# A hybrid encoder in fp32 on one core: the first output product in another PSUM bank, and loads, strips and stores put in another order

## The chip, the cores and the metric

One core of one Trainium2 chip. The metric is the device time of one execution in microseconds, the median of several runs. TensorE (PE, with its weight loads PEld) multiplies, VectorE (DVE) and ScalarE (ACT) work element by element, GpSimd (POOL) reduces over partitions, and SyncE (SP) issues the DMAs, in order, from one queue.

## The reference, cut to what matters

```python
def encoder_layer(h, norm_w, w_in, q_norm_a, k_norm_a, q_norm_b, k_norm_b, rpb, w_out, rope_tabs):
    B, N, _ = h.shape
    u = rms_norm(h, norm_w) @ w_in.astype(h.dtype)
    qa, ka, va, za, qb, kb, vb, zb = jnp.split(u, split_points(), axis=-1)
    qa = apply_axial_rope(rms_norm(qa.reshape(B, N, N_HEADS_A, HEAD_DIM), q_norm_a), rope_tabs)
    ka = apply_axial_rope(rms_norm(ka.reshape(B, N, N_KV_A, HEAD_DIM), k_norm_a), rope_tabs)
    va = va.reshape(B, N, N_KV_A, HEAD_DIM)
    ya = global_gqa(qa, ka, va) * jax.nn.silu(za)
    ...
    yb = neighbourhood_attention(qb, kb, vb, rpb) * jax.nn.silu(zb)
    y = jnp.concatenate([ya, yb], axis=-1) @ w_out.astype(h.dtype)
    return h + y
```

It is applied to a prompt of 1024 tokens and a sample of 256, each behind 16 meta tokens; the model has 2048 columns, 8 global heads (2 for K and V) and 8 local ones of 128 columns, all fp32. Global attention is softmax over all tokens, local attention over a window of 8 rows by 16 columns of a 64-wide grid, with a bias and the meta tokens.

## The kernel before, in words

Each fp32 operand is split into a high and a low fp32r half (`split`: ScalarE casts, L62; VectorE subtracts, L63), and a product is three matmuls (high by high, high by low, low by high).

*Projections.* A strip is one head's 128 columns of `w_in`. `strips` runs over 4 groups c of 4 row tiles kt; for each it loads the weights (tile wr, L190), splits them and multiplies (L211 to L213), for each block b of columns. Chunk 1 is 512 tokens: the sample, the meta tokens and the first 240 of the prompt. Chunk 2 is the other 784, in blocks of 512 (tiles x) and 272 (tiles xb), for which `load_all_x` (L145) loads all of x and keeps it split. A strip's sums lie in pool pp, four PSUM banks. They are read out by `qk_evac`, `v_rows`, with transposes on TensorE into pool tp, one bank (`v_turn` L261 and `rows_out` L502, copied out in L504 and L509), or `z_evac` (its first read is L267).

*Chunk 1* (L576) ends with the joint V and z strip of the last local head, whose rows are transposed in three turns through tp: the meta rows, split into vm (L63) and stored to vmd, the sample's rows, and the prompt's rows. vm is loaded again by `load_vm` for the values of that head. *Chunk 2* (L698) issues the loads of x, the rope tables (`consts`, L163) and the first k (`k_first`, L709), and begins with the joint strip of global K and V. In its global part two strips and the four query blocks of a head follow each other, and one strip of a local head fills in. Then `fill(len(late))` runs the other 24 late strips, in the order V, K, Q, z of each head; `run_due` is called at every second c, 48 times, and issues what `local_heads` has put at that place: loads of a head, the scores of a block, its values. `put_y` stores a block of y in L328. The last head's loads of k and q come due at place 46 of 48, its v and z follow the last strip, and its scores and values run between the first products.

*Output.* `outproj` (L1008) works through seven products of half-size matrices, 5 token tiles by 2 column blocks each: step n is 24 matmuls (`products`, L963) into pool pq, four banks that take over those of pp. w_out's operands take over the buffers of x (`w_load` L938: ww in xb; `w_operand` L949: wm in xa), and y's those of the strips' weights. From the second product on, `in_order` fixes the instructions of each engine in the order of the program. `load_y` and `make_y` get the y of tile m; from m = 10 on it is a sum of two loads (yr L904, ysum L930).

Apart from that, a planner orders instructions by the order of the program, by what is ready in its own model of time, and by the places where `issue_after`, `high_priority` or a dependency written by hand says otherwise. A pool with n buffers makes a tile wait for the release of the one n before.

## Time and profile before

| | us |
|---|---|
| median of 3 runs | 2173.62 (2173.07 to 2177.45) |
| profiled execution | 2173.82 |
| its span, first to last instruction | 2172.0 |
| first matmul; last strip matmul of chunk 1 starts | 5.35; 606.28 |
| last matmul of the strips starts | 1770.03 |
| first product starts | 1773.37 |

The mean granted TensorE clock is 0.999. A row of the timeline gives start, length, engine, line, operation, output<-inputs, sizes and count; a bracket gives the idle time of the engine before it and what ended it. A row of the waits gives who waited for whom, the total, the number and the longest. The time of a matmul in a row overlaps the next one's, so intervals are counted from start to start.

### The profile page before, as it was taken

To read this page: it belongs to the slowest core of one execution; us is meant where nothing else is said; L and a number is where in the kernel's file an instruction comes from. 1 tells how busy PE (TensorE), PEld (TensorE's weight loads), DVE (VectorE), ACT (ScalarE), POOL (GpSimd) and SP (SyncE) were. 2 spreads that over 40 slices of the span, in tenths; PEclk is the share of its full clock that TensorE was granted. 3 is DMA by queue.
4 is the path that set the end of the run, shared out by engine and by line. 5 is a ranking of instruction groups with operands and counts; after the bars stand their busy time and mean duration, and the time that the engine had idled before them with its cause. 6 is when DMAs were issued, how large, how long until landed. Compare 5 with 4: busy or idle time off the path is not lost.

```text
span 2172.0 us, 34106 instructions
## 1 busy us (share of the span) xinstructions
PE 2154.0 (99%) x11736; PEld 1879.0 (87%) x11736; DVE 1648.2 (76%) x2991; ACT 1113.5 (51%) x2294; POOL 523.4 (24%) x249
## 2 busy tenths in 40 slices
PE   9999999999999999999999999999999999999999
PEld 7888888888888999999999999989898988888887
DVE  8687976787864899997789988688777777455763
ACT  7556544555554666665666666444443464232230
POOL 1232422222311233231143224333333222000000
PEclk9999999999999999999999999999999999999999
DMA  8767889988554333334233344654433364663663
GB/s 301 222 198 230 281 285 322 348 276 264 176 187 145 103 110 106 116 115 139 98 115 98 109 131 143 188 160 139 135 124 121 125 202 133 219 241 102 232 224 107
DMA packets 263614, 383.83 MB, mean 177 GB/s; under 512 B 45040, under 2 KB 113296, under 8 KB 263440
## 3 DMA queue, kind: packets, MB, share of 16 engines
q1 hardware_dynamic: 263440, 381.65, 53.6%
q8 instruction: 92, 1.51, 0.3%
q14 instruction: 82, 0.67, 0.1%
HBM read 281.01 MB, written 100.38 MB: 176 GB/s over the span
## 4 chain that ended last, share of the span: by engine, by line
PE 90%; DVE 3%; DMA 3%; ACT 1%; issue 1%; SPq 1%; POOL 1%; DVEq 0%; ACTq 0%; POOLq 0%
PE pp L211 20%; PE pp L212 20%; PE pp L213 20%; PE pq L971 5%; PE pq L969 5%; PE pq L970 5%; PE sp L447 2%; PE po L481 1%; PE sp L343 1%; PE sp L342 1%; PE sp L341 1%; PE po L381 1%; PE po L382 1%; PE po L383 1%; PE tp L502 0%
## 5 line engine op out<-in xcount | busy, mean ns | idle before, releaser
L211 PE MATMUL pp<-x,wh 128*128 128x512 f32 (+1 forms) x1664 | 656.7, 396 | 5.4 <-ACT wh L62 5.3
L213 PE MATMUL pp<-x,wl 128*128 128x512 f32 (+1 forms) x1664 | 649.1, 390 | 0.0
L212 PE MATMUL pp<-x,wh 128*128 128x512 f32 (+1 forms) x1664 | 648.4, 390 | 0.0
L213 PEld LDWEIGHTS pp<-x,wl 128*128 128x128 f32 x1664 | 313.1, 188 | 62.3 <-DVE wl L63 0.9
L211 PEld LDWEIGHTS pp<-x,wh 128*128 128x128 f32 x1664 | 313.3, 188 | 61.8 <-ACT wh L62 6.3
L212 PEld LDWEIGHTS pp<-x,wh 128*128 128x128 f32 x1664 | 313.5, 188 | 52.6
L228 POOL PARTITION_ALL_REDUCE m<-ms x78 | 232.5, 2981 | 365.1 <-ACT ms L226 303.4
L63 DVE TENSOR_TENSOR wl<-wr,wh 128x512 fp32r<-128x512 f32 (+1 forms) x290 | 213.8, 740 | 126.0 <-ACT wh L62 103.2
L62 ACT CAST wh<-wr 128x512 fp32r<-128x512 f32 (+1 forms) x290 | 174.3, 606 | 216.8 <-PE pp L212 196.4
L310 POOL PARTITION_ALL_REDUCE tot<-a x80 | 177.1, 2214 | 445.2 <-DVE a L307 430.2
L212 PE MATMUL pp<-xb,wh 128*128 128x272 f32 x832 | 240.1, 289 | 0.0
L211 PE MATMUL pp<-xb,wh 128*128 128x272 f32 x832 | 239.6, 288 | 0.0
L213 PE MATMUL pp<-xb,wl 128*128 128x272 f32 x832 | 239.1, 287 | 0.0
L969 PE MATMUL pq<-wm,yh 128*128 128x512 f32 x560 | 219.2, 391 | 4.1 <-DVE z L267 3.1
L971 PE MATMUL pq<-wm,yl 128*128 128x512 f32 x560 | 218.9, 391 | 0.0
L970 PE MATMUL pq<-wm,yh 128*128 128x512 f32 x560 | 218.4, 390 | 0.0
L292 POOL PARTITION_ALL_REDUCE ma<-m x80 | 106.8, 1335 | 446.3 <-DVE m L290 441.7
L211 PEld LDWEIGHTS pp<-xb,wh 128*128 128x128 f32 x832 | 156.5, 188 | 7.3
L212 PEld LDWEIGHTS pp<-xb,wh 128*128 128x128 f32 x832 | 156.4, 188 | 7.1
L213 PEld LDWEIGHTS pp<-xb,wl 128*128 128x128 f32 x832 | 157.4, 189 | 0.1
L969 PEld LDWEIGHTS pq<-wm,yh 128*128 128x128 f32 x560 | 105.5, 188 | 26.4 <-ACT wm L62 3.2
L971 PEld LDWEIGHTS pq<-wm,yl 128*128 128x128 f32 x560 | 105.4, 188 | 22.3 <-DVE yl L63 0.4
(207 smaller groups left out, 3844.2 us busy)
## 6 DMA issues: line engine op xcount, KB each, us to landing
wr<-in_w_in SPq DMA_DIRECT2D x414, 256.0 KB, 3.4
wld<-wl SPq DMA_DIRECT2D x132, 256.0 KB, 4.3
wl<-wld SPq DMA_DIRECT2D x132, 256.0 KB, 3.1
yr<-yd SPq DMA_DIRECT2D x35, 512.0 KB, 5.2
wq<-in_w_out SPq DMA_DIRECT2D x64, 256.0 KB, 5.3
td<-wq SPq DMA_DIRECT2D x64, 256.0 KB, 4.3
ww<-td SPq DMA_DIRECT2D x64, 256.0 KB, 5.5
ww<-in_w_out SPq DMA_DIRECT2D x48, 256.0 KB, 5.1
```

Source lines behind the costliest of these rows:

```text
L62: self.hi = nc.scalar.copy(hi, full).ins
L63: return nc.vector.tensor_tensor(out=lo, in0=full, in1=hi.bitcast(F32), op=ALU.subtract).ins
L211: nc.tensor.matmul(p[:, :n], wh[:, k, :], xh[:, :n], start=first, stop=False)
L212: nc.tensor.matmul(p[:, :n], wh[:, k, :], xl[:, :n], start=False, stop=False)
L213: self.lastmm = nc.tensor.matmul(p[:, :n], wl[:, k, :], xh[:, :n], start=False, stop=last).ins
L228: nc.gpsimd.partition_all_reduce(m2[:], ms[:], P, RED.add)
L292: nc.gpsimd.partition_all_reduce(ma[:], m1[:], P, RED.max)
L310: nc.gpsimd.partition_all_reduce(tot[:], a1[:], P, RED.add)
L447: nc.tensor.matmul(dst, k[:, o:o + P], qfv[:, a:e, :], start=True, stop=True)
L969: nc.tensor.matmul(ps[:], yh, wh, start=k == 0, stop=False)
L970: nc.tensor.matmul(ps[:], yh, wl, start=False, stop=False)
L971: self.lastmm = nc.tensor.matmul(ps[:], yl, wh, start=False, stop=k == 7).ins
```

## The change

- Step 0 of the output product takes its PSUM tile from tp in place of pq.
- The last head's late strips run in the order K, Q, V, z; its k and q come due at place 44, its v at 46, its z after the strips. The loads of v and z are two functions now.
- The last strip, z, runs its two column blocks in turned order in every group c, and evacuates them so.
- Each local head's store of y gets a dependency on the last matmul before the next `run_due`; pool y has two buffers in chunk 2. Sl moves from pool sm (two buffers) into pool t, which gets a seventh.
- In chunk 2 the rope tables and the first k are issued on SP behind the first load of the last x; the weights of the first strip's groups 1, 2 and 3 and of the next strip's group 0 behind the loads of x of kt 3, 7, 11 and 15.
- The transposes of chunk 1's last strip are ordered behind the first block of 24 matmuls of chunk 2.
- y of tile 10 is loaded from step 16 on (before: step 18).

```diff
@@ load_all_x
                 with self.tc.issue_after(self.early):
-                    nc.sync.dma_start(r, self.x2d[kt][:, o:o + n])
+                    self.xload.setdefault(kt, nc.sync.dma_start(r, self.x2d[kt][:, o:o + n]).ins)
...
+        self.behind = [None] + [self.xload[c] for c in range(WCH - 1, KT, WCH)]
         for d, c in self.consts:
-            nc.sync.dma_start(d, c)
+            with self.tc.issue_after(self.xload[KT - 1]):
+                nc.sync.dma_start(d, c)
@@ strips
+            behind = self.behind.pop(0) if self.behind else None
             for s, _, _ in jobs:
-                with tc.high_priority(offset=self.woff):
+                with tc.high_priority(offset=self.woff), tc.issue_after(behind) if behind else nullcontext():
...
-            for b in range(len(jobs[0][1])):
+            nb = len(jobs[0][1])
+            for b in range(nb)[::-1] if self.turn else range(nb):
...
+                if self.second and self.turned:
+                    for i in self.turned:
+                        tc.add_manual_dep(i, self.lastmm.name, mybir.DependencyInfo(
+                            mybir.DependencyClass.NoSync, mybir.DependencyReason.DATA), reason="turned")
+                    self.turned = None
...
+    def turn_ins(self, i):
+        if not self.second:
+            self.turned.append(i)
...
     def run_due(self):
+        if self.late:
+            self.tc.add_manual_dep(self.late.pop(0), self.lastmm.name, mybir.DependencyInfo(
+                mybir.DependencyClass.Sync, mybir.DependencyReason.DATA), reason="late store")
@@ v_turn (rows_out in the same way)
-            self.nc.tensor.transpose(tp[:m, i, :], vt[:, o:o + m], self.ident[:])
+            self.turn_ins(self.nc.tensor.transpose(tp[:m, i, :], vt[:, o:o + m], self.ident[:]).ins)
@@ meta_scores
-        sm, sl = (self.sm.tile([M3, QB], F32, tag=n, name=n) for n in ("Sm", "Sl"))
+        sm = self.sm.tile([M3, QB], F32, tag="Sm", name="Sm")
+        sl = self.t.tile([P, QB], F32, tag="t", name="Sl")[:M3]
@@ put_y
-        nc.sync.dma_start(ydst, y[:].rearrange("p (g r) -> p g r", g=ydst.shape[1]))
+        self.ystore = nc.sync.dma_start(ydst, y[:].rearrange("p (g r) -> p g r", g=ydst.shape[1])).ins
@@ chunk1, before its last joint strip
+                self.turned = []
                 (v, vm), z = pr(vj, zj)
@@ chunk2
-            nc.sync.dma_start(k[:, :, :C1P].bitcast(F32), self.kd[g][:, :, :C1P])
-            nc.sync.dma_start(m.bitcast(F32), self.kd[g][:, :, C1P:])
+            with self.tc.issue_after(self.xload[KT - 1]):
+                nc.sync.dma_start(k[:, :, :C1P].bitcast(F32), self.kd[g][:, :, :C1P])
+                nc.sync.dma_start(m.bitcast(F32), self.kd[g][:, :, C1P:])
...
-                for p, (o, n) in zip(ps, BL):
+                for p, (o, n) in list(zip(ps, BL))[::-1 if self.turn else 1]:
...
         def values(h, b):
             next(blocks.pop((h, b)), None)
+            self.late.append(self.ystore)
...
-                    put(max(o + 5, 8 * h), load_vz, h + 1)
-            put(LATE - 2, load_kq, NH - 1)
+                    put(max(o + 5, 8 * h), load_v, h + 1)
+                    put(max(o + 5, 8 * h), load_z, h + 1)
+            put(LATE - 4, load_kq, NH - 1)
+            put(LATE - 2, load_v, NH - 1)
...
-            late += [v_rows_of(VB + h, 2 + h), qk_late(KB + h, kwb, self.k2d[2 + h]), qk_late(QB_ + h, qwb, self.q2d[8 + h]),
-                     z_late(ZB + h, self.zd[8 + h])]
+            v = [v_rows_of(VB + h, 2 + h)]
+            kq = [qk_late(KB + h, kwb, self.k2d[2 + h]), qk_late(QB_ + h, qwb, self.q2d[8 + h])]
+            late += (kq + v if h == NH - 1 else v + kq) + [z_late(ZB + h, self.zd[8 + h])]
...
-        fill(len(late))
-        load_vz(NH - 1)
+        fill(len(late) - 1)
+        self.turn = True
+        fill(1)
+        load_z(NH - 1)
@@ products
+        if first:
+            ps = self.tp.tile([P, 4, P], F32, tag="tp", name="pq")[:].rearrange("p a b -> p (a b)")
+        else:
+            ps = self.pq.tile([P, FB], F32, tag="pq", name="pq")[:]
@@ outproj
                 (load_y, make_y)[b](m + 1)
+                if m + 2 == 2 * NT:
+                    load_y(m + 2)
...
-            ps = self.products([ws[q, 8 * b + k] for k in range(8)], ys[m])
+            ps = self.products([ws[q, 8 * b + k] for k in range(8)], ys[m], n == 0)
@@ build
-                work = (("s", 5), ("ph", 2), ("sm", 2), ("mx", 2), ("t", 6))
+                work = (("s", 5), ("ph", 2), ("sm", 2), ("mx", 2), ("t", 7))
...
-                for name, bufs in (("k", 1), ("v", 1), ("tab", 1), ("q", 1), ("z", 1), *work, ("y", 1), ("qf", 1)):
+                for name, bufs in (("k", 1), ("v", 1), ("tab", 1), ("q", 1), ("z", 1), *work, ("y", 2), ("qf", 1)):
```

More of the change, by code (lines that the diff above doesn't have):

```diff
@@ L1 @@
-from contextlib import ExitStack
+from contextlib import ExitStack, nullcontext
 import numpy as np
@@ L145, in load_all_x @@
     def load_all_x(self):
-        nc = self.nc
+        nc, self.xload = self.nc, {}
         for kt in range(KT):
@@ L501, in rows_out @@
                 m = min(P, n - x)
-                nc.tensor.transpose(tp[:m, i, :], vt[:, x:x + m], self.ident[:])
+                self.turn_ins(nc.tensor.transpose(tp[:m, i, :], vt[:, x:x + m], self.ident[:]).ins)
             f = len(full)
@@ L577, in chunk1 @@
         nc, io = self.nc, self.io
-        self.due = iter(())
+        self.due, self.late, self.turn, self.behind, self.turned = iter(()), [], False, [], []
         self.woff, self.second, self.projected, self.sums = 0, False, 0, self.w_sums()
@@ L820, in run, with load_v, load_z @@
                 self.attend(q[:, :, c], z[:, c], keys, km, v, vm[:], self.yd[0][:, 2 * b:2 * b + 2, h, :])
-        kq, vz, blocks = {}, {}, {}
+        kqs, vs, zs, blocks = {}, {}, {}, {}
         def load_kq(h):
-            kq[h] = k_load(2 + h), self.bias_table(h, "bt", (3, 384)), q_load(8 + h)
-        def load_vz(h):
-            vz[h] = v_windows(h), z_load(8 + h)
+            kqs[h] = k_load(2 + h), self.bias_table(h, "bt", (3, 384)), q_load(8 + h)
+        def load_v(h):
+            vs[h] = v_windows(h)
+        def load_z(h):
+            zs[h] = z_load(8 + h)
         def scores(h, b):
-            (k, km), tab, (q, qf) = kq[h]
-            (v, vm), z = vz[h]
+            (k, km), tab, (q, qf) = kqs[h]
+            (v, vm), z = vs[h], zs[h]
             blocks[h, b] = self.attend_strip(q, qf, strips_of(z[:])[:, :, 64 * b:64 * b + 64], k, km, v[b], vm[:], tab, b,
@@ L838, in values @@
             next(blocks.pop((h, b)), None)
+            self.late.append(self.ystore)
         def local_heads():
             places = [[] for _ in range(LATE)]
-            seq = (values, load_vz, scores, load_kq)
+            seq = (values, load_v, load_z, scores, load_kq)
             def put(n, f, *a):
@@ L880, in chunk2 @@
                 fill(FILL)
-        load_kq(0)
-        load_vz(0)
+        for f in (load_kq, load_v, load_z):
+            f(0)
         self.due = iter(local_heads())
-        fill(len(late))
-        load_vz(NH - 1)
+        fill(len(late) - 1)
+        self.turn = True
+        fill(1)
+        load_z(NH - 1)
         self.due = iter([[(0, f, (NH - 1, b)) for f, b in ((values, n - 2), (scores, n)) if 0 <= b < 4] for n in range(6)])
@@ L961, in x_load, with products @@
         return o
-    def products(self, ws, y):
+    def products(self, ws, y, first):
         nc = self.nc
-        ps = self.pq.tile([P, FB], F32, tag="pq", name="pq")
+        if first:
+            ps = self.tp.tile([P, 4, P], F32, tag="tp", name="pq")[:].rearrange("p a b -> p (a b)")
+        else:
+            ps = self.pq.tile([P, FB], F32, tag="pq", name="pq")[:]
         for k in range(8):
@@ L968, in products @@
             yh, yl = (a[k // WCH][:, k % WCH, :] for a in y)
-            nc.tensor.matmul(ps[:], yh, wh, start=k == 0, stop=False)
-            nc.tensor.matmul(ps[:], yh, wl, start=False, stop=False)
-            self.lastmm = nc.tensor.matmul(ps[:], yl, wh, start=False, stop=k == 7).ins
-        return ps[:]
+            nc.tensor.matmul(ps, yh, wh, start=k == 0, stop=False)
+            nc.tensor.matmul(ps, yh, wl, start=False, stop=False)
+            self.lastmm = nc.tensor.matmul(ps, yl, wh, start=False, stop=k == 7).ins
+        return ps
     def out_sums(self, p, i, ps, o):
```

## The prediction

> **What bounds the kernel now.** I read the page first, then who TensorE waited for, then the stretches around each wait.

> ```profile
> span 2172.0 us, 34106 instructions
> ...
> PE 2154.0 (99%) x11736; PEld 1879.0 (87%) x11736; DVE 1648.2 (76%) x2991; ACT 1113.5 (51%) x2294; POOL 523.4 (24%) x249
> ```

> TensorE is busy for 2154.0 of 2172.0 us, so anything that is not a TensorE wait or a slowed matmul is worth nothing. The view of waits, TensorE alone (waiting engine and line, what ended the wait, total us, times, longest):

> ```profile
> PE pp L211 <- ACT wh L62: 5.3, 1, 5.3
> PE pq L969 <- DVE z L267: 3.1, 1, 3.1
> PE po L381 <- ACT ph L62: 1.6, 1, 1.6
> PE tp L261 <- DVE vm L63: 1.5, 1, 1.5
> PE sm_ps L280 <- DVE mx L351: 1.1, 2, 0.5
> PE pq L969 <- ACT yh L62: 1.0, 1, 1.0
> ```

> The first is the start of the program; the third and fifth belong to attention of chunk 1 and of the global heads, of which the diff moves one small tile (Sl) and nothing that is waited for. Three remain: L969 behind the last z evacuation, L261 behind the split of vm, L969 behind yh. What can be won is at these three places.

> **Place 1, the first product step** (the timeline of TensorE; start, length, what, and in brackets the idle time before it).

> ```profile
> 1769.90 0.29 PE L212 MATMUL pp<-xb,wh 128*128 128x272 f32 x1
> 1770.03 0.28 PE L213 MATMUL pp<-xb,wl 128*128 128x272 f32 x1
> 1773.37 0.77 PE L969 MATMUL pq<-wm,yh 128*128 128x512 f32 x1 [3.06 <-DVE z L267]
> ...
> 1776.90 0.40 PE L969 MATMUL pq<-wm,yh 128*128 128x512 f32 x1
> 1777.13 0.40 PE L970 MATMUL pq<-wm,yh 128*128 128x512 f32 x1
> ...
> 1780.34 0.60 PE L447 MATMUL sp<-qfull,kfull 128*128 128x128 f32 x4
> ...
> 1781.37 0.37 PE L281 MATMUL sp<-q,km 128*112 128x256 f32 x1 [0.31 <-DVE q L63]
> ```

> Matmuls overlap, so I count from start to start: 0.13 us for 272 columns (1769.90 to 1770.03), 0.23 us for 512 (1776.90 to 1777.13). The last projection matmul starts at 1770.03, the first product at 1773.37: 3.34 - 0.13 = 3.2 us lost. The step's 24 matmuls then take 1780.34 - 1773.37 = 6.97 us instead of 24 x 0.23 = 5.5, another 1.5. The stretches of time say why (length, each engine's busy time and instructions, then granted clock, DMA share and GB/s):

> ```profile
> 1770.00:1773.30 3.30, 0.31 (x3) 0.10 (x1) 3.30 (x7) 2.96 (x6) 0.00 (x0) 0.94 1.03 383
> 1773.30:1776.30 3.00, 2.93 (x7) 2.41 (x8) 2.85 (x5) 3.00 (x7) 0.00 (x0) 0.50 0.81 308
> ```

> After the idle 3 us the granted clock is 0.50 for the whole of the next 3. The 1.5 us hang on the wait and go with it. Last come 0.3 us in which the scores of the last head wait for q.

> What the change does here: step 0 (n == 0) writes the bank of the transposes instead of the first of the four banks that the projections give back, so it no longer waits for z to be read out of that bank. It needs that bank free, its operands, and then bank pq for step 1.

> The bank: the last V strip now ends one strip before the end, so its transposes stand in the z strip. How long they take is shown by the same head's V strip where it stands now (VectorE, then ScalarE):

> ```profile
> 1708.15 0.69 DVE L254 TENSOR_TENSOR vt<-pp,rb 128x512 f32<-128x512 f32 x1
> ```

> ```profile
> 1717.03 0.25 ACT L509 COPY vl<-tp 16x128 f32<-16x128 f32 x1
> ```

> From the first vt to the last copy out of the bank: 9.1 us. A strip is 48 x (0.23 + 0.13) = 17.3 us by the intervals above, so the bank is free some 8 us before step 0. If that cover were gone, step 0 would wait as now (a rival).

> The operands: VectorE has the low halves of w_out and y to make.

> ```profile
> 1772.54 0.69 DVE L267 TENSOR_TENSOR z<-pp,rb 128x512 f32<-128x512 f32 x1
> ...
> 1777.60 0.68 DVE L63 TENSOR_TENSOR wm<-ww,wm 128x512 fp32r<-128x512 f32 x1
> ...
> 1779.40 0.43 DVE L267 TENSOR_TENSOR z<-pp,rb 128x272 f32<-128x272 f32 x1
> ```

> The last of 16 wm is done at 1778.28. Unstalled, step 0 runs from 1770.2 to 1775.7, the scores of the last head to about 1777.0, and step 1 takes its last weight 21 x 0.23 = 4.8 us later, at 1781.8: 3.5 us to spare even at today's times. They will be earlier: Q's evacuation and the split of q leave this stretch for the strip before, V puts less work on VectorE, and with the blocks turned round the 272-column blocks of x, whose buffers the w_out loads take over, come free 12 x 0.23 = 2.8 us sooner per group of four; the 512-column ones come free 12 x 0.13 = 1.6 us later, but only the casts behind the loads need them. Turning costs no matmul. With Q a strip (17 us) earlier, the 0.3 us wait for q goes too.

> Step 1 now takes the first of pq's four banks, the one that step 0 waits for today, so z's 512-column block must be read by 1777.0. Today that block comes first, is complete at about 1770.0 - 12 x 0.13 = 1768.5, and is read from 1772.54, 4.0 us later. Turned, it is complete at 1770.3 and by the same delay read out by 1775.0, 2 us in time. I take no wait; the far bound is the place of today's second z block, done at 1779.83, a wait of 2.8.

> Sum of place 1: 3.2 + 1.5 + 0.3 = **5.0 us**, at least 2.2.

> [...]

> **Place 2, where chunk 2 starts.**

> ```profile
> 607.80 0.28 PE L261 MATMUL tp<-ident,vt 128*16 128x128 f32 x1
> 609.59 0.44 PE L261 MATMUL tp<-ident,vt 128*128 128x128 f32 x2 [1.51 <-DVE vm L63]
> ```

> The two transposes share one bank; the second waits until VectorE has split vm. The change orders all transposes of this strip behind the first 24 matmuls of chunk 2 (K and V, four kt, 512 columns: 5.5 us), and puts the loads of x ahead of k, of the rope tables and of later weights on SP. What TensorE has at 607.8 instead: 24 matmuls of 272 columns, whose x landed earlier, 3.1 us; then the 512-column ones as x arrives. ScalarE's rows for the casts of x:

> ```profile
> 609.18 0.72 ACT L159 ACTIVATE x<-x,nw 128x512 fp32r<-128x512 f32 x1 [0.61 <-DMA x<-x2d]
> ...
> 613.88 0.72 ACT L159 ACTIVATE x<-x,nw 128x512 fp32r<-128x512 f32 x1 [2.83 <-DMA x<-x2d]
> ```

> The first x is cast at 609.90 and TensorE would reach it at 610.9: covered. The third is late now because stores of vm and two weight loads stand ahead of it on SP; the stores move behind the transposes and the loads behind x. I take the full **1.5 us**. If the third x stays where it is, TensorE runs out at 610.9 + 12 x 0.23 = 613.7, and idles until 614.6, and as long again if the fourth follows as late, 1.8 us in place of 1.5: bounds -0.3 and +1.5. What moves back on SP: k and rope, first used in evacuations some 35 us later (two strips), which hides them; two weight loads by two issues, with 5.5 + 3.1 us of matmuls ahead of their use. The store of vm and its reload move some 5.5 us later, ahead of the last sample head's values; these are placed later by as much, and nothing of chunk 2 needs them soon.

> **Place 3, the third pass of products.**

> ```profile
> 1905.26 0.39 PE L971 MATMUL pq<-wm,yl 128*128 128x512 f32 x1
> 1906.67 0.50 PE L969 MATMUL pq<-wm,yh 128*128 128x512 f32 x1 [1.02 <-ACT yh L62]
> 1907.00 0.40 PE L970 MATMUL pq<-wm,yh 128*128 128x512 f32 x1
> 1907.39 0.50 PE L971 MATMUL pq<-wm,yl 128*128 128x512 f32 x1
> ```

> Three intervals take 2.13 us instead of 0.69: 1.4 lost. The cause is upstream on VectorE:

> ```profile
> 1889.20 1.23 DVE L930 TENSOR_TENSOR ysum<-yr 128x1024 f32<-128x1024 f32 x1 [4.58 <-DMA yr<-yd]
> ```

> VectorE stands 4.58 us for y of tile 10, with 16 wm and the next ysum queued behind it. The change issues this load at step 16 instead of 18, two steps or 11 us earlier. The queue moves up by up to 4.58 us, over three times what TensorE lost: **1.4 us**. Below, 0: it would take a load that, issued 11 us earlier, still kept VectorE waiting all 4.58 us. The order of instructions is fixed here by hand, so nothing else moves.

> **What costs nothing.** Late y stores: a store on SP waits for a later matmul; behind it stand weight loads. Between 1326 and 1733 TensorE is busy all the time,

> ```profile
> 1326.00:1733.00 407.00, 407.00 (x2445) 367.11 (x2444) 312.70 (x664) 187.01 (x421) 138.69 (x74) 1.00 0.45 144
> ```

> although SP already waits 84.4 us in all with these stores at its head:

> ```profile
> SPq L328 <- DVE y L327: 84.4, 42, 5.2
> ```

> The second y buffer and the seventh t are paid for with the two buffers of Sl; off TensorE's path either way: 0, bounds -1.1 (a pair of 0.5 waits for mx more) and +1.1 (both gone).

> **Sum.** 5.0 + 1.5 + 1.4 = 7.9 us off the profiled execution's 2173.8 (its span of 2172.0 and 1.8 around it) gives 2165.9; that execution stands 0.2 above the median of the runs, so as a median **2165.7 us**.

> **Rivals.** (a) *The wait moves to step 1*: VectorE comes to z's 512-column block as late as to today's second block. For it: VectorE is busy for 3.30 of 3.30 us there. Against: Q's work is gone from the stretch. 2.8 back: 2168.5, with half clock again, 1.5 more, 2170.0. (b) *x is the wait at chunk 2's start*: place 2 gives nothing or loses 0.3: 2167.2 to 2167.5. For it: the casts waited 2.83 us for x. Against: what stood ahead of it moves. (c) *The bank of the transposes isn't free*, so step 0 starts as late as today: 5.0 back, 2170.7. For it: V's evacuation now competes with the w_out splits. Against: 8 us of slack. (d) *Slower*: from 1326 on, 28 late stores hold SP until the matmul they are tied to, weights behind them come late, and TensorE waits once per store. It decides from 7.9 / 28 = 0.28 us per store; at 0.5, the longest wait for mx, it costs 14: 2179.7. For it: SP is in order. Against: the row of full TensorE under 84.4 us of held SP.

> **How the numbers follow.** Forecast 0.54, (b) 0.15, (a) 0.13, (d) 0.10, (c) 0.08. A measurement of this kernel can tell about 0.2%, 4.3 us, from no change: faster means below 2169.3. The forecast and (b) lie there nearly whole (0.67), (a) by half (0.07): 0.74. Slower is (d): 0.10; the rest, 0.16, within. The range begins at 2163.5 (the forecast less 1.1 for mx and 1.2 for other small waits) and ends at 2171.5, above (a) and (c); (d) is left out, and a tenth for what I haven't thought of.

> **What would show it.** Step 0 starting at about 1768.7 right behind the last z matmul, granted clock 1.00 through the stretch, no L447 or L281 wait; no wait at L261 and none for x around 608; no wait for yh in the third pass and none of VectorE for yr. A wait for z at step 1, one for x at L211, or any TensorE wait between 1326 and 1733 would make it wrong.

## The result

| | median, us (range) | runs |
|---|---|---|
| before, same chip | 2175.48 (2172.71 to 2178.41) | 20 |
| changed | 2172.49 (2170.73 to 2176.40) | 20 |
| predicted | 2165.7 (2163.5 to 2171.5) | |

The ratio is 0.9986, 95% interval 0.998 to 0.9992: 3.0 us faster, or 0.14%, where 7.9 us were forecast. The direction was right, the size was not. The profiled execution of the changed kernel took 2173.16 us, 0.7 more than its median; the one of before lies at the low end of its runs. So the traces differ by less than the medians, and are read for places, not for their total.

The page, and TensorE's waits (waiting engine and line, what ended the wait, total us, times, longest):

```profile
span 2171.4 us, 34104 instructions
...
PE 2154.0 (99%) x11736; PEld 1879.1 (87%) x11736; DVE 1647.0 (76%) x2991; ACT 1117.0 (51%) x2294; POOL 526.5 (24%) x249
```

```profile
...
PE tp L519 <- ACT wm L62: 3.9, 1, 3.9
...
PE pp L215 <- ACT x L159: 1.1, 1, 1.1
PE tp L519 <- DVE vt L270: 0.5, 1, 0.5
```

The waits that the prediction set out to remove are gone: the products' for z and for yh (L969), chunk 2's for vm (L261) and the scores' for q; with them went the scores' for mx (L280). In their place stand one for x and one, longer than any of them, at the transposes of the last V strip. The changed kernel's lines lie 4 to 31 further down: 211 to 213 are 215 to 217, 254 is 270, 261 is 277, 502 is 519, 504 is 521, 969 to 971 are 1000 to 1002.

**The new stand.** The timeline around it, all engines (start, length, engine, line, what; idle time before in brackets):

```profile
1752.38 0.32 SPq L821 DMA_DIRECT2D qfull<-q2d  x1
...
1757.41 0.28 PE L215 MATMUL pp<-xb,wh 128*128 128x272 f32 x1
1757.89 1.04 ACT L62 CAST q<-qfull 128x1024 fp32r<-128x1024 f32 x1 [3.47 <-DMA qfull<-q2d]
1758.84 0.61 ACT L62 CAST wh<-wr 128x512 fp32r<-128x512 f32 x1
1758.97 1.23 DVE L63 TENSOR_TENSOR q<-qfull,q 128x1024 fp32r<-128x1024 f32 x1 [3.56 <-ACT q L62]
1759.36 0.58 ACT L521 COPY vl<-tp 128x512 f32<-128x512 f32 x1
...
1760.11 0.69 DVE L63 TENSOR_TENSOR wl<-wr,wh 128x512 fp32r<-128x512 f32 x1
...
1760.71 0.42 DVE L340 TENSOR_TENSOR y<-po,z 128x256 f32<-128x256 f32 x1
1761.05 0.43 DVE L270 TENSOR_TENSOR vt<-pp,rb 128x272 f32<-128x272 f32 x1
...
1761.63 0.66 PE L519 MATMUL tp<-ident,vt 128*128 128x128 f32 x2 [3.93 <-ACT wm L62]
```

Read it from the bottom. TensorE stands 3.93 us in the middle of the z strip, at the second group of V's transposes. The view names wm as what ended it; but a transpose needs its input vt and the bank tp, and vt is what is late, done at 1761.48. Before it on VectorE's queue stands the split of q, which waits 3.56 us for ScalarE's cast of q. On ScalarE that cast stands in front of the copy that empties the bank (L521), and waits 3.47 us for the load of q, issued at 1752.38 and there at 1757.8. So both engines stood idle at the head of their queues for q, which the scores take up only at 1781.9, and V's evacuation, due at once, stood behind.

The stretches behind it (length, each engine's busy time and instructions, then granted clock, DMA share, GB/s):

```profile
1757.00:1760.30 3.30, 0.69 (x6) 0.48 (x4) 1.33 (x2) 2.41 (x4) 0.00 (x0) 1.00 0.37 123
1760.30:1763.70 3.40, 2.07 (x9) 2.02 (x10) 3.32 (x7) 1.57 (x4) 0.00 (x0) 0.51 0.59 172
1763.70:1767.20 3.50, 3.50 (x9) 2.69 (x9) 1.65 (x3) 1.80 (x5) 0.00 (x0) 0.50 0.95 304
1767.20:1770.60 3.40, 3.40 (x22) 3.01 (x21) 2.32 (x4) 2.12 (x4) 0.00 (x0) 1.00 1.06 369
```

Before had one stretch of 3.4 us at half clock, behind the first product's wait; here are two. The first product itself now follows without a gap, 0.23 us behind the last matmul of the strips:

```profile
1776.20 0.39 PE L217 MATMUL pp<-x,wl 128*128 128x512 f32 x1
1776.43 0.39 PE L1000 MATMUL pq<-wm,yh 128*128 128x512 f32 x1
```

At chunk 2's start TensorE waits for the cast of x. ScalarE's rows show why that cast is late:

```profile
608.32 0.38 ACT L414 ACTIVATE Sm<-sm_ps 48x256 f32<-48x256 f32 x1 [6.17 <-PE sm_ps L412]
608.60 2.55 ACT L159 ACTIVATE x<-x,nw 128x512 fp32r<-128x512 f32 x4
...
609.36 0.73 PE L215 MATMUL pp<-x,wh 128*128 128x512 f32 x2 [1.08 <-ACT x L159]
```

The first x was issued at 603.34 and landed 2.8 us later, at 606.1. But on ScalarE its cast stands behind Sm, the read of the last sample head's meta scores, and Sm waits 6.17 us for TensorE's own matmuls. So x is there, and its cast is late by the order of ScalarE's queue.

In the third pass VectorE gets y of tile 10 with no wait (before, it stood 4.58 us), and the products run through:

```profile
1885.48 1.22 DVE L958 TENSOR_TENSOR ysum<-yr 128x1024 f32<-128x1024 f32 x1
...
1906.43 0.39 PE L1000 MATMUL pq<-wm,yh 128*128 128x512 f32 x1
1906.66 0.39 PE L1001 MATMUL pq<-wm,yh 128*128 128x512 f32 x1
```

What each place loses in a trace, in us: the sum over its matmuls of the interval to the next start, less the usual interval of that shape. "Again" is a second profiled execution of the changed kernel.

| place | before | changed | again |
|---|---|---|---|
| last strips and first products | 5.7 | 7.9 | 5.7 |
| chunk 2's start | 2.6 | 2.1 | 2.1 |
| two waits for mx (780, 1117) | 2.2 | 0.7 | 0.7 |
| third pass | 1.5 | -0.1 | -0.1 |

So the change gains 3.6 us at three places and nothing, or less, where 5.0 were forecast.

### The profile page after: what moved, and what is told of

Read it like the earlier page. It is cut to its first block, busy times and chain, and to the rows that moved or that the text cites. A ratio compares the mean times of both kernels' runs of the same rounds, so it can differ in the third digit from the quotient of the medians.

```text
span 2171.4 us, 34104 instructions
## 1 busy us (share of the span) xinstructions
PE 2154.0 (99%) x11736; PEld 1879.1 (87%) x11736; DVE 1647.0 (76%) x2991; ACT 1117.0 (51%) x2294; POOL 526.5 (24%) x249
## 3 DMA queue, kind: packets, MB, share of 16 engines
q8 instruction: 92, 1.51, 0.3%
## 5 line engine op out<-in xcount | busy, mean ns | idle before, releaser
L244 POOL PARTITION_ALL_REDUCE m<-ms x78 | 224.4, 2877 | 355.3 <-ACT ms L242 317.1
L63 DVE TENSOR_TENSOR wl<-wr,wh 128x512 fp32r<-128x512 f32 (+1 forms) x290 | 215.8, 746 | 116.9 <-ACT wh L62 98.7
L327 POOL PARTITION_ALL_REDUCE tot<-a x80 | 184.5, 2306 | 443.3 <-DVE a L324 415.1
L62 ACT CAST wh<-wr 128x512 fp32r<-128x512 f32 (+1 forms) x290 | 175.0, 606 | 213.5 <-PE pp L216 194.9
```

The lines of the kernel that those rows point to most:

```text
L62: self.hi = nc.scalar.copy(hi, full).ins
L63: return nc.vector.tensor_tensor(out=lo, in0=full, in1=hi.bitcast(F32), op=ALU.subtract).ins
L244: nc.gpsimd.partition_all_reduce(m2[:], ms[:], P, RED.add)
L327: nc.gpsimd.partition_all_reduce(tot[:], a1[:], P, RED.add)
```

## The experiments

Three theories at first. **T**: the early load of q puts its cast in front of V's evacuation; the stand and the half clock hang on that order. **Rival A**: V's strip now lies where w_out is cast, so its bank comes free late with or without q. **Rival B**: the late stores make q land late. Kernels ran in four groups, each on a chip of its own beside runs of before (medians 2177.4 to 2177.8), so ratios are compared across groups and times within one.

**q behind V's copies.** The cast of the last head's q is queued behind the last copy of its V rows, and its k and q come due at place 46 in place of 44:

```diff
-                nc.scalar.copy(t[:], tp[:m, f, :])
+                self.lastvl = nc.scalar.copy(t[:], tp[:m, f, :]).ins
...
+            with self.tc.issue_after(self.lastvl) if h == NH - 1 else nullcontext():
+                kqs[h] = *kt, q_load(8 + h)
...
-            put(LATE - 4, load_kq, NH - 1)
+            put(LATE - 2, load_kq, NH - 1)
```

> The changed kernel with one thing added: ScalarE's cast of the last head's q is queued behind the last copy of that head's V rows (vl). Theory T (in the changed kernel the cast of q, which waits for its load, stands at the head of ScalarE's queue in front of the copies that free the transposes' bank, and its split on VectorE stands in front of the second vt): TensorE's stand of 3.9 us before the second group of V's transposes goes and with it most of the 6.8 us at half clock; 7 us less than the changed kernel, about 10 us less than before (2165 where before has 2175). Rival A (V's strip now lies where w_out is cast, and the bank would come free late with or without q): a wait of 2 us or more stays at the transposes, and at most 3 us are gained on the changed kernel.

Measured: 2172.65 us against 2177.42, ratio 0.9978 (0.997 to 0.9987). TensorE's waits (lines here are two further down), then SP's issues and ScalarE's cast of y:

```profile
PE pq L1002 <- ACT yh L62: 2.1, 1, 2.1
PE tp L519 <- DVE vt L270: 1.5, 2, 0.8
```

```profile
1769.03 2.46 SPq L767 DMA_DIRECT2D vw<-vn  x4
1771.54 0.50 SPq L940 DMA_DIRECT2D yl<-yd  x1
...
1776.38 0.62 ACT L62 CAST yh<-yl 128x512 fp32r<-128x512 f32 x1 [1.62 <-DMA yl<-yd]
```

The load of q is still issued just ahead of the first transposes (1754.72, against 1754.85; 0.1 us ahead in the changed kernel too), so what differs is the order on ScalarE. The stand at the second transposes is gone; only 0.8 for the first vt of the strip is left there. Rival A falls. In this execution q landed 3.5 us after issue, which by the table further down is worth a stand of some 1.7 us, not 3.9. The time gained over the changed kernel is near 1 us by the ratios, not 7, for a new wait came up: the first product, after 12 of its 24 matmuls, waits 2.1 us for the second half of its y, whose load SP issued behind the four loads of V windows. Nor is the half clock gone for good: the profiled execution has none ahead of the last 5 us, but the mean granted clock is 1.00 in only 5 of the 12 runs. T was right on the order that makes the stand, and wrong on its price and on what follows it.

**V first.** The old order of the last head's strips:

```diff
-            put(LATE - 4, load_kq, NH - 1)
+            put(LATE - 2, load_kq, NH - 1)
...
-            late += (kq + v if h == NH - 1 else v + kq) + [...]
+            late += (v + kq) + [...]
```

> The changed kernel with the last head's strips in the old order V, K, Q, z and the load of its k and q in the old place; bank, late stores, x loads and y load are as in the changed kernel. T: no stand at the transposes, since V's evacuation lies two strips ahead of the load of q; some 7 us less than the changed kernel, less up to 0.5 us if the scores of the last head wait for q as they did before (2165 to 2166 where before has 2175). Rival A expects the same here; it parts from T in the run with q behind V. A rival by which the order of strips is worth its 3 us on its own (the products' first step waits again): 2168 or more, with a wait at step 0.

Measured: 2170.87 us, ratio 0.997 (0.9959 to 0.9981). No wait at the transposes and none at step 0, but the last head's scores now wait for q, and a stretch of 3.4 us at half clock follows:

```profile
PE sp L464 <- DMA qfull<-q2d: 1.9, 1, 1.9
```

That is 6.5 us less than before on its chip, where T said 9 to 10. By the ratios the new order of strips gains nothing over the old one as it stands: 0.997 with the old one, 0.9986 and, further down, 0.9982 with the new, though the intervals overlap.

**No late stores.** `self.late.append(self.ystore)` taken out.

> The changed kernel without the late y stores of the local heads (each store is queued as early as the order allows, as before). Rival B (the late stores lie on SP's queue and in the transfer engines beside the load of q, and so q lands only 5.4 us after its issue): q lands about 3 us after issue, the stand of 3.9 us falls to 1.5 us or less, 3 us or more are gained on the changed kernel. T: the load of q takes about as long, the stand stays within 1 us of 3.9, and the time within 1.5 us of the changed kernel's (2171 to 2174 where before has 2175); the two waits for mx around 780 and 1117 may come back (0.7 us each).

Measured: 2170.81 us, ratio 0.9969 (0.9957 to 0.9981). q lands 3.3 us after issue, the longest wait at the transposes is 1.4 us, no half clock before the end. These are rival B's numbers, not T's: by the ratios an edit that the prediction priced at zero costs some 3 us. The two waits for mx stay away.

**The bank alone.** The kernel before, with step 0 in the transposes' bank and nothing else:

```diff
+        if first:
+            ps = self.tp.tile([P, 4, P], F32, tag="tp", name="pq")...
...
+            ps = self.products([...], ys[m], n == 0)
```

> The kernel before with one edit: the first product step accumulates in the transposes' bank. By the prediction's first term: no idle time ahead of step 0 (3.06 us before) and no window at half clock there; 4.7 us less than before. If the wait only moves to step 1: 1.5 to 3 us less. If the bank isn't free: no difference.

Measured: 2177.92 us, ratio 1.0 (0.9992 to 1.0009). Step 0 doesn't wait any more, but (SP's issue, then TensorE):

```profile
1780.22 0.32 SPq L802 DMA_DIRECT2D qfull<-q2d  x1
...
1783.47 1.83 PE L447 MATMUL sp<-qfull,kfull 128*128 128x128 f32 x6 [3.93 <-DMA qfull<-q2d]
```

```profile
1782.00:1785.40 3.40, 1.93 (x7) 1.96 (x8) 2.98 (x5) 2.52 (x6) 0.00 (x0) 0.52 0.39 146
1785.40:1789.00 3.60, 3.60 (x11) 2.91 (x11) 1.14 (x3) 0.69 (x2) 0.00 (x0) 0.51 0.02 5
```

The bank was free, the time fits "no difference" all the same: the wait moved to the scores, for q, 3.9 us with 6.8 us of half clock behind. In the trace of before this wait was 0.3 us, because the wait for z covered the rest. It is why the change needs q early at all.

**The changed kernel again**, on the chip of the next three.

> The changed kernel once more, beside the others on one chip. T: a stand at the second group of V's transposes, its length set by when the last head's q lands: 3.9 us when q lands 5.4 us after issue (as profiled first), about 1.5 us when it lands 3.3 us after issue (as in the run without late stores, which has the same order on ScalarE and VectorE). Time 2.5 to 7 us less than before, by the length of the stand and the half clock behind it.

Measured: 2174.23 us against 2177.75, ratio 0.9982 (0.9973 to 0.999). q lands 4.9 us after issue, the stand is 3.4 us, one stretch at half clock. Over all kernels with q ahead of V's copies, in order of the landing:

| kernel | late stores at the end | q, issue to landing, us | stand at the second transposes, us |
|---|---|---|---|
| no late stores | no | 3.3 | 1.4 |
| late stores but the last head's | no | 3.3 | 1.4 |
| late stores of the last head only | yes | 3.5 | 1.7 |
| x loads as before | yes | 3.6 | 1.8 |
| transposes not turned | yes | 3.7 | 1.9 |
| changed, again | yes | 4.9 | 3.4 |
| changed | yes | 5.4 | 3.9 |

(Left out: the two kernels with one y buffer, where TensorE already stood 2.0 us at the first transposes and came later to the second.) Each row is one execution. One us more of landing is 1.2 us more of stand (from the first row to the last 2.1 and 2.5). With the run "q behind V's copies", where q landed after 3.5 us and nothing stood at the second transposes, that settles the cause of the stand; why the load takes 3.3 us in one execution and 5.4 in another isn't settled. The late store issued within a us behind it goes with the slow ones, but loads with it range from 3.5 to 5.4.

**Both.** q behind V's copies and no late stores.

> The changed kernel with the cast of the last head's q behind V's copies and without the late y stores. With q behind V alone the wait moved on to the second product step, whose y was loaded behind the four loads of the last head's V windows; here that y goes ahead of them. T with this addition: neither a stand at the transposes (under 1 us in all) nor a wait of the products for y; no half clock before the last 5 us of the span; 2 us less than with either edit alone, 8 to 9 us less than before. Rival: the transfers themselves bound the stretch (the four V loads and w_out share the engines), a wait of 1.5 us or more comes up at some product step or at the last head's scores, and nothing is gained on either edit alone.

Measured: 2169.38 us (2168.05 to 2170.22), ratio 0.996 (0.9947 to 0.9972): 8.4 us less than before, 4.9 less than the changed kernel on the same chip. SP issues y now ahead of V's windows, and the only wait at the transposes in the whole span is short:

```profile
1767.79 0.38 SPq L939 DMA_DIRECT2D yl<-yd  x1
...
1769.25 2.80 SPq L767 DMA_DIRECT2D vw<-vn  x4
```

```profile
PE tp L519 <- DVE vt L270: 0.4, 1, 0.4
```

The place loses 1.4 us in all (5.7 before). (The text above calls it the second product step; it is the second half of the first.) The square of the two edits, as ratios: 0.9982 to 0.9986 with both, 0.9978 without q ahead, 0.9969 without late stores, 0.996 with neither. Neighbouring intervals overlap; those of the two corners do not.

**Where the late stores cost.** Late stores for all but the seventh local head (`if h < NH - 2:` ahead of the append), and for the seventh alone (`if h == NH - 2:`); its stores fall into the last strips.

> The changed kernel with late stores for all local heads but the seventh, whose stores fall into the last strips; the order of SP's queue there is that of the run without late stores. If the late stores cost by what they do at the end (a store right behind the load of q, and the V loads ahead of y): q lands 3.3 to 3.5 us after issue, the stand at the second transposes is 1 to 2 us, no wait at step 1; 2170 to 2171.5 where before has 2177.5, as without any late store (ratio 0.997). If 24 stores cost by holding SP along the strips: as the changed kernel, 2173 to 2174 (0.998 to 0.9985).

> The complement: late stores for the seventh local head alone. If they cost by what they do at the end: as the changed kernel, a stand of 2 to 4 us at the second transposes, half clock in most executions, ratio 0.998 to 0.9985. If by holding SP along the strips: as without late stores, 0.997.

Measured: 2169.91 us (2168.93 to 2171.44), ratio 0.9969 (0.9958 to 0.998), and 2171.99 us (2170.85 to 2173.47), ratio 0.9975 (0.9967 to 0.9984), on one chip. The first is as without late stores, so by themselves the other 24 cost nothing, as forecast; the last four cost 2.1 us. The second's forecast was missed on the rest: its stand is 1.7 us, and the granted clock was 1.00 in all 11 of its runs, where half clock was expected in most. The changed kernel, which has both parts, had 1.00 in 6 of 31 runs and ratios of 0.9982 and 0.9986, on other chips; so the half clock takes something that neither part shows alone, and what that is stays open. TensorE's waits in the second, which the first has not or smaller (its stand is 1.4, and no product waits):

```profile
PE tp L519 <- ACT wm L62: 1.7, 1, 1.7
PE pq L1001 <- ACT yh L62: 1.4, 1, 1.4
```

What differs in the traces is the place of y on SP, behind V's windows, and the stand, a little longer with q's landing. With late stores at the end and a stand of 2 us or less, five kernels of six wait 0.5 to 2.1 us for that y; with q ahead or behind and no late stores there, none of the three named does.

**One y buffer; buffers as before.** First `("y", 1)` in chunk 2; then also Sl back in its own tag of sm and `("t", 6)`.

> The changed kernel with one y buffer in the second chunk, as before, and its other buffers as changed. If the second y buffer took away the two waits of a scores' start for mx (0.7 us each at 780 and 1117 before), they come back and the time is 1.4 us more than the changed kernel's; if it was the other edits of buffers (Sl in the shared pool with a seventh buffer), they stay away and the time is within 0.5 us.

> The changed kernel with all its buffers as before: Sl in its own tag of the sm pool, six buffers in the shared pool and one y in chunk 2. With one y alone the two waits for mx (0.7 us each) stayed away. If Sl and the seventh buffer took them away they are back here (around 780 and 1117), 1.4 us more than the changed kernel; if neither, they stay away and come from the late stores or the order of x, and the time is within 0.5 us.

Measured: 2173.49 us, 0.9978 (0.9969 to 0.9987), no wait for mx; and 2173.64 us, 0.9982 (0.9973 to 0.999), with this row back:

```profile
PE sm_ps L296 <- DVE mx L368: 1.1, 2, 0.5
```

The pair went with Sl and the seventh buffer, 1.5 us by the table. The time doesn't show it, against a kernel whose stand and half clock vary as the changed one's do: the granted clock was 1.00 in 8 of the 11 runs with the old buffers, in 2 of the 11 of the changed kernel. The second y buffer has a use too: with one, the first transposes wait 2.0 us for vt in both kernels, against 0.5 in the changed one.

**Chunk 2's start.** Transposes not turned behind the first products, and x loads as before:

> The changed kernel without the edit that puts the last head's transposes of chunk 1 behind chunk 2's first products; x loads, weights and k are as changed. T: with the transposes first TensorE waits for vm again at 608 (1.5 us, as before) and the wait for x (1.1 us) goes or shrinks; 0.4 to 0.8 us more than the changed kernel. If x were late on its own the two waits would stand one behind the other: 1.5 us more.

> The changed kernel with the x loads of chunk 2 in their old place among weights and k; the transposes stay turned behind the first products. If the x loads are what gained at chunk 2's start: TensorE waits 2 us or more for x around 609, where the changed kernel waits 1.2, and the time is 1 us or more above the changed kernel's. If the turned transposes are: the wait stays at 1.2 us.

Measured: 2171.42 us, 0.997 (0.9959 to 0.9982), and 2173.86 us, 0.9985 (0.9976 to 0.9994). The waits there, of the first and of the second kernel:

```profile
PE tp L277 <- DVE vm L63: 0.7, 1, 0.7
```

```profile
PE pp L213 <- ACT x L159: 1.9, 1, 1.9
```

The place loses 1.7 us without the turning, 2.9 without the x loads, 2.1 changed, 2.6 before. The x loads gain 0.8: in their old place the first x lands at 610.6, behind Sm. The turning trades 0.7 for vm against 1.1 for x and loses 0.3. The times bear out neither forecast. Without the turning 0.4 to 0.8 us more was expected, and it was 2.8 less on the same chip; its tail differs too (q landed 3.7 us after issue), so the difference can't be put down to the turning. With the x loads as before 1 us or more above the changed kernel was expected, and the ratio of 0.9985 is that of the changed kernel.

**The third term alone.** In the kernel before, `load_y(m + 2)` a step earlier where m + 2 is the tenth tile.

> The kernel before with one edit: the y of the tenth tile is loaded a step earlier in the third pass of products. The prediction's third term: the wait of 1.2 us at step 22 goes, the products run without a gap, 1.2 to 1.6 us less than before; 0 if the load was late for another reason than its place.

Measured: 2176.33 us, ratio 0.9994 (0.9986 to 1.0003). The trace shows the gap gone (1.5 to -0.1); the time fell by 1.3 us, which this interval cannot tell from none.

**A version without the three edits that cost** (q behind V, no late stores, transposes not turned):

> The changed kernel with the cast of the last head's q behind V's copies, without the late y stores and without the edit that turns the transposes behind chunk 2's first products. T: as the run with the first two of these, with a wait of 1.0 us in place of the 1.2 us for x at 609; within 1 us of that run, 8 to 9 us less than before. Rival: what the late stores and the turned transposes guard against shows up elsewhere, and 2 us or more are lost against that run.

Measured: 2170.23 us, ratio 0.9964 (0.995 to 0.9977): as the kernel of both, which stays the fastest seen. Its start of chunk 2 is 0.3 us better, and a wait of 1.0 us at the last head's scores, for za, takes that back.

## Why the prediction was wrong

**Place 1 (5.0 us forecast; 0 to -2 in the traces): the step that failed.** The wait for z went, step 0 began right behind the strips, and step 1 found its bank, as worked out. What failed is the sentence "Q's evacuation and the split of q leave this stretch for the strip before". It was counted as relief for where they leave; nobody asked what they meet where they go. They meet V's evacuation, on both engines, with a load to wait for. And "the bank is free some 8 us before step 0" asked only for the last user of the bank. The transposes themselves are matmuls in TensorE's queue between those of z: V's evacuation could be late without touching step 0, and stop TensorE 15 us ahead of it. Rival (c) named the right competitor, V's evacuation against other work on the same engines, but for step 0, with the w_out splits, and dismissed it by the slack of 8 us. One more part of the step was not looked at: of the operands the prediction timed w_out's (wm), not the second half of the first product's y. In the changed kernel, where the stand makes the first product late, nothing waits for it; in "q behind V's copies" it cost 2.1 us.

**The 0.3 us for q was mis-sized.** With the bank alone it is 3.9 us and 6.8 at half clock. The row of before showed what was left of a wait behind a longer one. The sum is not off by it, since the change loads q early.

**Late stores (0): 2 to 3 lost.** Their cover was read from the stretch 1326 to 1733, where TensorE is full, and rival (d) asked for a price per store over all 28. By themselves the first 24 cost nothing. Three of the last four are issued behind 1733, where SP's queue holds q, y and V at once; that end was left out of the view.

**Buffers (0, upper bound 1.1): 1.5.** The waits were known and the gain allowed as a bound; what went with each was 0.7, not the 0.5 of idle time that the row gives: the first, in before, takes 0.83 us from start to start (779.55 to 780.38) where 0.13 is usual, and the row counts only from the end of the matmul ahead, 0.28 after its start.

**Place 2 (1.5): 0.5.** TensorE waits 1.1 us for x, as rival (b) said, but not for its reason. The prediction had TensorE run 24 matmuls of 272 columns first, 3.1 us of cover, and rival (b) feared a late load of the third x. In the trace the matmuls of the first x, 512 columns wide, come first, and its cast, 2.5 us after the landing, stands behind Sm on ScalarE. So again what failed is the order on an engine's queue. The gain is from the x loads alone; what a cast ahead of Sm would bring wasn't run.

**Place 3 (1.4): 1.6**, right in place and cause.

Put together: 7.9 less 5.0 to 7.2 at place 1, where the price of the late stores lies too, less 1.0 at place 2, plus 1.5 from the buffers and 0.2 at place 3, leaves 1.4 to 3.6; the medians say 3.0 and 3.5. With q's cast behind V's copies and no late stores the gain is 8.4 us, with place 1 at 1.4 us lost in place of 5.7. That it matches the 7.9 is partly luck: places 1 and 2 give 4.3 and 0.6 of their 6.5, and the 1.5 from the buffers, not in the sum, make up for the rest. The clock in the runs agrees: 1.00 in 4 of 20 and 2 of 11 runs of the changed kernel, in all 7 and all 5 of the kernels "late stores but the last head's" and "both".

## What to carry to other kernels

When a step is moved earlier, look at the queues where it arrives: a load's first consumer that stands ahead of urgent work on an engine's queue can make that work wait for the load, as the cast of q did here, where ScalarE, busy for 51% of the span, stood 3.47 us; so put such a consumer behind the evacuation it might hold up. A wait that follows a longer wait is measured by taking the longer one away (the wait for q: 0.3 us in its row, 3.9 with the wait for z gone), not by its row. A step called free because its queue has slack on average is to be asked about its worst place, here the last four of 28 stores.

## What the runs showed of the hardware

Idle time and half clock do not go together by the length of a wait alone. 3.93 us of standing gave 6.8 us at half clock in two kernels (changed, and the bank alone), 3.4 (changed, again) and 3.06 us (before) gave 3.4; 1.9 us gave 3.4 at the scores of "V first" (its granted clock falls at 1779.5), while 2.1 us in "q behind V's copies" and 1.9 at the transposes of "not turned" gave none. What tells them apart in these traces is where the wait lies. In before and changed the clock changes in steps of 3.413 us: ahead of the last 5 us half clock lasted 3.41 us in before and 6.83 in changed, and full clock up to it 1761.28 (516 steps) and 1751.04 (513). Cut a trace into windows of that length, counted from a change of the clock, and the idle time within one window sorts these cases, each window at full clock itself:

| kernel | window from, us | TensorE idle in it, us | clock in the next window |
|---|---|---|---|
| third term alone | 1773.81 | 1.7 | 1.00 |
| transposes not turned | 1756.87 | 1.8 | 1.00 |
| x loads as before | 609.55 | 1.8 | 1.00 |
| V first | 1776.10 | 1.9 | 0.50 |
| third term alone | 609.87 | 1.9 | 0.50 |
| changed, again | 1758.95 | 2.3 | 0.50 |
| before | 1769.51 | 2.6 | 0.50 |

The wait of 2.1 us in "q behind V's copies" is cut into 1.3 and 0.8 by the edge of a window, and the wait of 2.98 us before the first product of "the third term alone" into 1.7 and 1.3; no half clock followed. That the edges fell so by chance is the author's estimate. The 7 of 12 runs of the former with a clock below 1.00 would fit a less lucky cut, but were not traced.

The load of q, 392 KB, issued at the same point of the queue, landed 3.3 to 5.4 us after issue from one execution to the next. TensorE's stand followed it at 1.2 to 1; how much of the spread of the runs, 2170.7 to 2176.4, comes from there wasn't measured.
